# Token count in its own PSUM bank, and GpSimd work taken off the second layer's routing

## The chip, the cores and the metric

The kernel runs on one core of one Trainium2 chip. The metric is the device time of one execution in microseconds (us); before the change it was 1033.38 us, the median of three runs (1032.68 to 1035.6). In the profile, PE is the matrix engine (PEld its weight loads), DVE the vector engine, ACT the scalar engine, POOL is GpSimd, SP issues the weight loads.

## The reference, cut to what matters

512 tokens of 1024 float32 numbers pass through two layers. Each is a mixer, a layer norm, a mixture of 16 experts of which a token uses two, and another layer norm.

```python
for i in range(DEPTH):                                   # DEPTH = 2
    ...                                                  # mixer i, memory attention -> tok, xa
    o = jnp.concatenate([tok, xa], axis=-1) @ w_out[i]
    x = layer_norm(ALPHA * x + o, ln1_g[i], ln1_b[i])
    f = grouped_moe(x, router_w, router_b, w_gate[i], w_up[i], w_down[i])
    x = layer_norm(ALPHA * x + f, ln2_g[i], ln2_b[i])

# grouped_moe
scores = sigmoid(xt @ router_w); sel = scores + router_b
# the group with the largest sum of its two best sel, then its two best experts
combine = ...                                            # normalised gates, 2 per token
for e in range(N_EXPERTS):                               # 16
    h = silu(xt @ w_gate[e]) * (xt @ w_up[e])
    out = out + combine[:, e:e + 1] * (h @ w_down[e])
```

## The kernel before

**Arithmetic.** A float32 operand is used as a high part (a rounded copy, made by ACT) and a low part (value minus high part, made by DVE). Each product is three matmuls: high by high, high by low, low by high (`mm3`). Weights come in loads of 1 MB (`raw`), issued by SP in a fixed order. `Stream.split` (L155) turns one load into either two pages `split` (2 x 128x1024) or a pair `high`, `low` (128x2048). A load can start when a page is free, and the loads in flight are limited.

**Routing** (`route`, L528). After the first layer norm, the four blocks of 128 rows are written to two DRAM tensors, `x1d` (rows to gather) and `rd` (the residual to which the experts add), by DMAs on POOL's queue. PE makes the logits, and DVE ranks them in small instructions, first for blocks 0 to 2 and then for block 3. PE counts positions (`pos`). DVE compares the positions with 1 to 128 (`sel`, 128x128, by `choose`, L618), and PE multiplies `sel` by the token numbers and gates, which accumulates the table `tab`: for each of the 16 experts, up to 128 token numbers and gates. `tables` (L631) makes `idxs` and `gates` from it.

**Overflow** (`overflow`, L598). PE sums how many tokens each expert has (`cnt`), DVE compares with 128, 256 and 384 (`ovf`), sums, and writes the flags and the number `nover` of full extra blocks. All five engines read `nover` (L893) and jump over a rarely used loop (L894, `more`) if it is 0, as here. Each does so in its own order of instructions; nothing behind the jump starts before it on that engine.

**Experts** (`experts`, L651). A page `xg` of two row blocks is zeroed by POOL (L655), since a gather leaves rows without a token alone. Then POOL gathers the rows of experts 0 and 1 (L668). In layer 0, the *fillers* behind the table are the last quarter of the next layer's value projection (`va`); in layer 1 they are 8 matmuls whose results nobody uses (`warm`, L299). After the jump PE transposes `xg` (`xt`, L677), ACT and DVE make its parts `xgt`, and the expert's products follow: `ga` and `ua`, transposes `htr`, then `ya`.

**What sets the order.** Before the jump, a list scheduler places the instructions of each engine; `issue_after` forbids it to place one ahead of another. Behind the jump, `manual_schedule` keeps PE, ACT and DVE in the order of the program text. Tiles of tag "R" share one PSUM bank: `lg`, `tab` and `cnt` follow each other in it. Tag "B" has three banks.

Of the kernel before, what the change touches and what calls it, by code (L numbers as in the profile page):

```python
# [22 lines left out]
AF = mybir.ActivationFunctionType  # L23
OP = mybir.AluOpType
AX = mybir.AxisListType
ET = mybir.EngineType

P = 128
D = 1024
KB = D // P  # L30
S = 512
NC = S // P
# [3 lines left out]
E = 16  # L36
# [11 lines left out]
def trunk(ctx, tc, x, mem, w_in_a, sgu_ln_g, sgu_ln_b, sgu_w, sgu_b, w_in_b, conv_w, w_kv, w_out,  # L48
          ln1_g, ln1_b, router_w, router_b, w_gate, w_up, w_down, ln2_g, ln2_b, out):
    nc = tc.nc  # L50
    vec, act, pool_e, pe, sp = nc.vector, nc.scalar, nc.gpsimd, nc.tensor, nc.sync
# [12 lines left out]
    def page(name, shape, dtype=FT, of=None):  # L64
        of = free_pages if of is None else of
        assert of, f"no page for {name}; held: {sorted(v[1] for v in held.values())}"
        i = of.pop(0)
        uid[0] += 1
        t = pages.tile(shape, dtype, name=f"{name}_{uid[0]}", tag=f"pg{i}", bufs=1)
        held[id(t)] = (i, name, t)  # L70
        return t

    def drop(*ts):
        for t in ts:
            i, name, _ = held.pop(id(t))
            W.home(name).append(i)
# [4 lines left out]
    def bank(shape, name="bank"):  # L81
        return psum.tile(shape, FT, name=name, tag="B", bufs=3)

    def tiny(n, name):
        return psum.tile([P, n], FT, name=name, tag="R", bufs=1)


    class Half:


        def __init__(self, high, low, *pages):
            self.high, self.low, self.pages = high, low, pages
# [5 lines left out]
    class Stream:  # L98
        def __init__(self):
            self.todo, self.raw, self.ready = [], [], []  # L100
            self.keep, self.ahead, self.stop, self.sent = 0, 4, 0, 0
            self.hold, self.whole, self.count, self.on_pool = False, False, 0, lambda n: False
            self.after, self.behind, self.loads, self.flight = None, None, [], 2
            self.spare, self.parts = free_pages, 0

        def rings(self, n):
# [48 lines left out]
        def split(self):  # L155
            t, h = self.raw[0]
            if self.whole and not h:
                high, low = (page(n, [P, 4, 512], FR, self.spare) for n in ("high", "low"))
                src = t
                self.ready += [Half(high[:, 0:2], low[:, 0:2]), Half(high[:, 2:4], low[:, 2:4], high, low)]  # L160
                self.raw[0][1] = 2
            else:
                g = page("split", [P, 2, 2, 512], FR, self.spare)
                src, high, low = t[:, 2 * h:2 * h + 2], g[:, 0], g[:, 1]
                self.ready.append(Half(high, low, g))
                self.raw[0][1] += 1
            with ExitStack() if self.after is None else tc.issue_after(self.after):
                act.activation(high, src, AF.Copy)  # L168
            (pool_e if self.on_pool(self.count) else vec).tensor_tensor(low, src, high, op=OP.subtract)  # L169
            self.count += 1  # L170
            if self.raw[0][1] == 2:
                self.raw.pop(0)
                drop(t)
# [24 lines left out]
    W = Stream()  # L198

    def mm3(o, a, b, start, stop):  # L200
# [2 lines left out]
        pe.matmul(o, a[0], b[1], start=False, stop=False)  # L203
        return pe.matmul(o, a[1], b[0], start=False, stop=stop)  # L204

    def split_to(hi, lo, src):
        r = act.activation(hi, src, AF.Copy)  # L207
        vec.tensor_tensor(lo, src, hi, op=OP.subtract)  # L208
        return r


# [39 lines left out]
    ones_b = consts.tile([P, P], BF, name="ones_b")  # L251
# [16 lines left out]
    thr = consts.tile([P, 3 * E], FT, name="thr")  # L268
# [26 lines left out]
    def keep_warm(n):  # L295

        t = bank([P, 4, P], "warm")
        for _ in range(n):
            pe.matmul(t, ones_b, ones_b[:, None, :].to_broadcast([P, 4, P]), start=True, stop=True)  # L299
# [54 lines left out]
    def project_t(xh, xl):  # L354

        a = [acc("za") for _ in range(4)]
        for j in range(4):
            g = W.next()
            for kk in range(2):
                k = 2 * j + kk  # L360
                for b in range(4):
                    cs = slice(b * P, (b + 1) * P)
                    mm3(a[b], (g[:, 0, kk, cs], g[:, 1, kk, cs]), (xh[k // 4][:, k % 4, :], xl[k // 4][:, k % 4, :]),
                        k == 0, k == KB - 1)
            W.done(g)
        return a
# [141 lines left out]
    nover = consts.tile([1, 1], I32, name="nover")  # L508
# [3 lines left out]
    oh = consts.tile([P, NC, E], BF, name="oh")  # L512
# [85 lines left out]

    def overflow():

        cnt = tiny(E, "cnt")
        for c in range(NC):
            pe.matmul(cnt, ones_b, oh[:, c], start=(c == 0), stop=(c == NC - 1))
        f = small.tile([1, E, 3], FT, name="ovf", bufs=1)
        vec.tensor_tensor(f, cnt[0:1, :, None].to_broadcast([1, E, 3]),
                          thr[0:1].rearrange("p (e j) -> p e j", j=3), op=OP.is_gt)
        no = small.tile([1, 1], FT, name="ovn", bufs=1)
        vec.tensor_reduce(no, f.rearrange("p e j -> p (e j)"), axis=AX.X, op=OP.add)
        vec.tensor_copy(flags, f.rearrange("p e j -> p (e j)"))
        vec.tensor_copy(nover, no)  # L610

    tab, last_entry = [], []
    idxs = consts.tile([P, E], I32, name="idxs")
    gates = consts.tile([P, E], FT, name="gates")

# [15 lines left out]
    def tables():  # L631

        t = tab[0].rearrange("p (e t) -> p e t", t=3)
        vec.tensor_scalar(idxs, t[:, :, 0], 1.0, None, op0=OP.subtract)
        return vec.tensor_reduce(gates, t[:, :, 1:3], axis=AX.X, op=OP.add)

    def table(pp, rhs):

# [12 lines left out]
    def experts(i, lnp, fill, after, stop, fine=False):  # L651

        last = E - 1
        xg = page("xg", [P, 2, D])
        pool_e.memset(xg, 0.0)  # L655
        hy = page("h", [P, 4, FE])
        hp = hy[:, 0:2]
        xt = page("xgt", [P, 2, KB, P], FR)
# [8 lines left out]
        def gather(e):  # L667
            pool_e.indirect_dma_start(out=xg[:, e % 2], out_offset=None, in_=x1d[i],  # L668
                                      in_offset=bass.IndirectOffsetOnAxis(ap=tabs[e][0], axis=0),
                                      bounds_check=S - 1, oob_is_err=False)  # L670

        def xtrans(e):
            for q in range(2):
                t = bank([P, 4, P], "xt")
                for k in range(4):
                    k0 = 4 * P * q + 2 * P * (k // 2) + k % 2
                    pe.transpose(t[:, k, :], xg[:, e % 2, k0:k0 + 2 * P - 1:2], ident)  # L677
                split_to(xt[:, 0, 4 * q:4 * q + 4, :], xt[:, 1, 4 * q:4 * q + 4, :], t)
# [41 lines left out]
        gather(0)  # L720
        gather(1)
        if i:
            with tc.issue_after(last_entry[-1]):
                keep_warm(8)
        fill()
        more(i, hy)
# [2 lines left out]
        W.rings(8)  # L729
        xtrans(0)  # L730
        gather(2)
        W.pump()
        order = ExitStack()
        order.enter_context(tc.manual_schedule(engines={ET.PE, ET.Activation, ET.DVE}))
        for e in range(E):
# [15 lines left out]
            if e == last:  # L751
# [5 lines left out]
                t = bank([P, NC, P], "selt")  # L757
# [213 lines left out]
    stop = -len(W.todo) - W.sent  # L971
# [20 lines left out]
    t = bank([P, 12], "cwt")  # L992
    pe.transpose(t, cwr, ident[:12, :12])
    act.activation(cw.rearrange("p t b -> p (t b)"), t, AF.Copy)
    t = bank([P, H, P], "sgt")
# [7 lines left out]
    a = project_t(xh, xl)  # L1003
# [6 lines left out]
    a = project(xh, xl)  # L1010
# [5 lines left out]
    a = project_t(xh, xl)  # L1016
# [25 lines left out]
    def mixer_end(i, ch, cl, lnp):  # L1042
        lg = [tiny(3 * E, "lg"), None]

        def after(c, normed):
            if c == 0:
                W.on_pool = (lambda n: n % 2 == 1) if i == 0 else (lambda n: n % 3 != 0)
                W.keep, W.ahead = (2, 3) if i == 0 else (1, 2)
                W.pump()
            if c == NC - 1:  # L1050
                lg[1] = bank([P, E], "lg3")
                lg.append(normed)
            logits(c, i, lg[1] if c == NC - 1 else lg[0][:, c * E:(c + 1) * E])
            if c % 2:
                drop(xs[c // 2])
            if c == 1:
                W.pump()
        project_out(i, ch, cl, lnp, after)
        drop(lnp)
        rp = page("route", [P, 2048])  # L1060
        route(0, 3, lg[0].rearrange("p (n e) -> p n e", e=E), lg[2], rp)
        route(3, 1, lg[1].rearrange("p (n e) -> p n e", e=E), lg[2], rp)
        tables()
        drop(rp)
        overflow()
        W.ahead = 4

    mixer_end(0, ch, cl, lnp)
    kv1 = []
    W.keep = 6  # L1070
# [20 lines left out]
    a = project_halves(xh, xl)  # L1091
# [7 lines left out]
    a = project_t(xh, xl)  # L1099
    for h in range(H):  # L1100
        act.activation(cgp[:, h, :], a[h], AF.Copy)
    a = project_t(xh, xl)
# [7 lines left out]
    a = project_t(xh, xl)  # L1110
# [10 lines left out]
    W.keep = 3  # L1121
    mixer_end(1, ch, cl, lnp)
    W.keep = 6
    W.pump()

    def store(c):
        for n in range(2):
            ns = slice(n * 512, (n + 1) * 512)
            sp.dma_start(out[0, c * P:(c + 1) * P, ns], xrow[c][:, ns])
    experts(1, (ln2_g[1], ln2_b[1]), lambda: None, store, 0, fine=True)  # L1130


# [26 lines left out]
```

## Time and profile before

| | |
|---|---|
| median of 3 runs | 1033.38 us (1032.68 to 1035.6) |
| profiled execution, its own time | 1031.97 us |
| its span | 1030.1 us, 12721 instructions |
| PE busy | 983.7 us (95%) |
| DVE busy | 774.2 us (75%) |
| ACT busy | 627.7 us (61%) |
| POOL busy | 200.5 us (19%) |
| read from HBM | 262.22 MB |

The busy time of an engine is the sum of its instructions; matmuls are pipelined, so a busy PE can still be slow. The granted clock is a share of PE's full speed: 1.00 is 2.4 GHz, 0.50 is 1.2 GHz. The span is cut into 40 slices of 25.75 us on the page; PE is under 90% in six of them: the first, the last, one at 206 us and three from 670 to 747 us, where the experts of a layer begin.

### The profile page before, as it was taken

To read this page: it belongs to the slowest core of one execution; us is meant where nothing else is said; L and a number is where in the kernel's file an instruction comes from. 1 tells how busy PE (TensorE), PEld (TensorE's weight loads), DVE (VectorE), ACT (ScalarE), POOL (GpSimd) and SP (SyncE) were. 2 spreads that over 40 slices of the span, in tenths; PEclk is the share of its full clock that TensorE was granted. 3 is DMA by queue.
4 is the path that set the end of the run, shared out by engine and by line. 5 is a ranking of instruction groups with operands and counts; after the bars stand their busy time and mean duration, and the time that the engine had idled before them with its cause. 6 is when DMAs were issued, how large, how long until landed. Compare 5 with 4: busy or idle time off the path is not lost. (4 is left out here: it accounts for less than half of the span.)

```text
span 1030.1 us, 12721 instructions
## 1 busy us (share of the span) xinstructions
PE 983.7 (95%) x4815; PEld 810.6 (79%) x4816; DVE 774.2 (75%) x884; ACT 627.7 (61%) x684; POOL 200.5 (19%) x111
## 2 busy tenths in 40 slices
PE   8999999969999999999999999977899999999995
PEld 6788888858888888888679887865688888888873
DVE  4738567867989898898894455675689898988975
ACT  4626532556788787878643414233687887878763
POOL 0000002112332413321110000221133324233023
PEclk9999999989999999999999999987899999999998
DMA  9813266667999999999880425490799999999944
GB/s 321 294 42 123 91 237 247 244 225 265 364 367 333 366 360 360 360 357 362 282 320 1 164 82 207 131 396 25 232 330 362 372 327 383 359 362 355 357 87 160
DMA packets 102219, 273.30 MB, mean 265 GB/s; under 512 B 10442, under 2 KB 10966, under 8 KB 102152
## 3 DMA queue, kind: packets, MB, share of 16 engines
q1 hardware_dynamic: 89480, 242.84, 64.5%
q0 software_dynamic: 11808, 26.97, 9.4%
q10 hardware_dynamic: 864, 2.62, 0.7%
q8 instruction: 39, 0.64, 0.2%
q14 instruction: 28, 0.23, 0.1%
HBM read 262.22 MB, written 26.21 MB: 280 GB/s over the span
## 5 line engine op out<-in xcount | busy, mean ns | idle before, releaser
L169 DVE TENSOR_TENSOR low<-raw,high 128x2048 fp32r<-128x2048 f32 x189 | 427.9, 2288 | 80.9 <-ACT high L168 79.4
L168 ACT ACTIVATE high<-raw 128x2048 fp32r<-128x2048 f32 x189 | 355.1, 1910 | 22.7 <-PE ga L204 10.1
L668 POOL DMA_INDIRECT xg<-x1d,idxs x32 | 83.2, 2601 | 299.6 <-PE xt L677 270.5
L168 ACT ACTIVATE split<-raw 128x1024 fp32r<-128x1024 f32 x66 | 68.9, 1058 | 71.1 <-PE za L204 26.0
L202 PE MATMUL ya<-high,ht 128*128 128x512 f32 x256 | 103.8, 406 | 0.0
L169 DVE TENSOR_TENSOR split<-raw,split 128x1024 fp32r<-128x1024 f32 x61 | 73.6, 1221 | 39.6 <-ACT split L168 38.9
L204 PE MATMUL ga<-high,xgt 128*128 128x512 f32 x248 | 99.1, 399 | 2.9 <-DVE xgt L208 2.9
L204 PE MATMUL ya<-high,ht 128*128 128x512 f32 x256 | 101.3, 396 | 0.1
L203 PE MATMUL ya<-low,ht 128*128 128x512 f32 x256 | 101.1, 395 | 0.0
L202 PE MATMUL ga<-high,xgt 128*128 128x512 f32 x248 | 100.7, 406 | 0.1
L203 PE MATMUL ga<-low,xgt 128*128 128x512 f32 x248 | 98.4, 397 | 0.0
L204 PE MATMUL ua<-high,xgt 128*128 128x512 f32 x248 | 97.1, 392 | 0.0
L202 PE MATMUL ua<-high,xgt 128*128 128x512 f32 x248 | 96.9, 391 | 0.0
L203 PE MATMUL ua<-low,xgt 128*128 128x512 f32 x248 | 96.8, 390 | 0.0
L169 POOL TENSOR_TENSOR split<-raw,split 128x1024 fp32r<-128x1024 f32 x5 | 11.9, 2383 | 267.0 <-DVE sto L475 147.0
L202 PE MATMUL za<-xh,split 128*128 128x512 f32 x160 | 61.6, 391 | 2.0 <-ACT xh L207 2.0
L203 PE MATMUL za<-xl,split 128*128 128x512 f32 x160 | 62.5, 391 | 0.0
L204 PE MATMUL za<-xh,split 128*128 128x512 f32 x160 | 61.5, 389 | 0.0
L204 PEld LDWEIGHTS ga<-high,xgt 128*128 128x128 f32 x248 | 47.4, 191 | 14.1 <-DVE xgt L208 4.0
L204 PEld LDWEIGHTS ya<-high,ht 128*128 128x128 f32 x256 | 48.1, 188 | 12.8 <-DVE ht L208 1.3
L664 POOL DMA_INDIRECT rd<-h,idxs x16 | 40.4, 2523 | 89.3 <-ACT h L718 79.6
L202 PEld LDWEIGHTS ya<-high,ht 128*128 128x128 f32 x256 | 48.4, 189 | 10.5 <-ACT ht L207 0.6
(250 smaller groups left out, 1886.2 us busy)
## 6 DMA issues: line engine op xcount, KB each, us to landing
raw<-in_w_gate_dram SPq DMA_DIRECT2D x64, 1024.0 KB, 9.8
raw<-in_w_up_dram SPq DMA_DIRECT2D x64, 1024.0 KB, 9.6
raw<-in_w_down_dram SPq DMA_DIRECT2D x64, 1024.0 KB, 10.5
raw<-in_w_kv_dram SPq DMA_DIRECT2D x8, 1024.0 KB, 7.4
raw<-in_w_out_dram SPq DMA_DIRECT2D x8, 1024.0 KB, 8.0
raw<-in_w_in_b_dram SPq DMA_DIRECT2D x8, 1024.0 KB, 11.1
raw<-in_w_in_a_dram SPq DMA_DIRECT2D x6, 1024.0 KB, 5.4
x1d<-x POOLq DMA_DIRECT2D x8, 512.0 KB, 6.0
```

The costliest lines, as they stand in the source:

```text
L168: act.activation(high, src, AF.Copy)
L169: (pool_e if self.on_pool(self.count) else vec).tensor_tensor(low, src, high, op=OP.subtract)
L202: pe.matmul(o, a[0], b[0], start=start, stop=False)
L203: pe.matmul(o, a[0], b[1], start=False, stop=False)
L204: return pe.matmul(o, a[1], b[0], start=False, stop=stop)
L664: added[e] = pool_e.indirect_dma_start(out=rd[i], out_offset=bass.IndirectOffsetOnAxis(ap=tabs[e][0], axis=0), in_=ys[e % 2], in_offset=No ...
L668: pool_e.indirect_dma_start(out=xg[:, e % 2], out_offset=None, in_=x1d[i], in_offset=bass.IndirectOffsetOnAxis(ap=tabs[e][0], axis=0), bou ...
```

## The change

1. `cnt` gets a tile of tag "B" instead of sharing the bank of `tab`, so its matmuls no longer wait until `gates` has been read. In layer 1 the fillers must now come behind the last `cnt` matmul. The four DVE instructions of the count are placed behind `gates`.
2. In layer 1, ACT zeroes `xg` with a scaled copy of ones, where POOL did it.
3. In layer 1, the low parts of the splits placed around the routing are all made by DVE, behind the write of `nover`.
4. At the start of `experts`, in both layers, the low parts that `pump` makes there are placed behind the second low part of the first rows (`xgt`).

```diff
-            (pool_e if self.on_pool(self.count) else vec).tensor_tensor(low, src, high, op=OP.subtract)
+            with ExitStack() if self.low_after is None else tc.issue_after(self.low_after):
+                (pool_e if self.on_pool(self.count) else vec).tensor_tensor(low, src, high, op=OP.subtract)
...
     def split_to(hi, lo, src):
         r = act.activation(hi, src, AF.Copy)
-        vec.tensor_tensor(lo, src, hi, op=OP.subtract)
+        last_low[:] = [vec.tensor_tensor(lo, src, hi, op=OP.subtract).ins]
...
-        cnt = tiny(E, "cnt")
+        cnt = bank([P, E], "cnt")
         for c in range(NC):
-            pe.matmul(cnt, ones_b, oh[:, c], start=(c == 0), stop=(c == NC - 1))
+            m = pe.matmul(cnt, ones_b, oh[:, c], start=(c == 0), stop=(c == NC - 1))
...
+        with tc.issue_after(tabbed[0]):
+            vec.tensor_tensor(f, cnt[0:1, :, None].to_broadcast([1, E, 3]),
+                              thr[0:1].rearrange("p (e j) -> p e j", j=3), op=OP.is_gt)
...
-        vec.tensor_copy(nover, no)
+        return m.ins, vec.tensor_copy(nover, no).ins
...
-        pool_e.memset(xg, 0.0)
+        if i:
+            act.activation(xg.rearrange("p a d -> p (a d)"), ones_b[:, 0:1].to_broadcast([P, 2 * D]), AF.Copy, scale=0.0)
+        else:
+            pool_e.memset(xg, 0.0)
...
-            with tc.issue_after(last_entry[-1]):
+            with tc.issue_after(counted[0]), tc.issue_after(last_entry[-1]):
                 keep_warm(8)
...
+        W.low_after = last_low[0]
         W.pump()
+        W.low_after = None
...
     mixer_end(1, ch, cl, lnp)
     W.keep = 6
+    W.low_after, W.on_pool = counted[1], lambda n: False
     W.pump()
+    W.low_after = None
```

On DVE in layer 0, from the table to the jump, this stood before (`low` are weights of expert 0, `vt` values of the next layer's attention):

```order
L634 TENSOR_SCALAR idxs<-tab 128x16
L635 TENSOR_REDUCE gates<-tab 128x16
L169 TENSOR_TENSOR low_2081<-raw_1310,high_2080 128x2048
L169 TENSOR_TENSOR low_2057<-raw_1254,high_2056 128x2048
L208 TENSOR_TENSOR vt_1701<-va,vt_1701 128x512
L605 TENSOR_TENSOR ovf<-cnt,thr 1x48
L208 TENSOR_TENSOR vt_1701<-va,vt_1701 128x512
L608 TENSOR_REDUCE ovn<-ovf 1x1
L609 CAST flags<-ovf 1x48
L610 CAST nover<-ovn 1x1
L893 TENSOR_LOAD nover
```

In the changed kernel the same place on DVE reads:

```order
L638 TENSOR_SCALAR idxs<-tab 128x16
L639 TENSOR_REDUCE gates<-tab 128x16
L609 TENSOR_TENSOR ovf<-cnt,thr 1x48
L612 TENSOR_REDUCE ovn<-ovf 1x1
L613 CAST flags<-ovf 1x48
L614 CAST nover<-ovn 1x1
L170 TENSOR_TENSOR low_2081<-raw_1310,high_2080 128x2048
L211 TENSOR_TENSOR vt_1701<-va,vt_1701 128x512 x2
L902 TENSOR_LOAD nover
```

The count moved ahead of one `low` and both `vt`; the other `low` went behind the jump and behind both `xgt` low parts. With it one load of SP, which reuses that page, went behind the jump.

On POOL in layer 1, from the last rows to the jump, this stood before:

```order
L516 DMA x1d_114<-x_4275 128x1024
L517 DMA rd_116<-x_4275 128x1024
L169 TENSOR_TENSOR split_5889<-raw_5061,split_5889 128x1024
L655 MEMSET xg_5892 128x2048
L668 DMA xg_5892<-x1d_114,idxs 128x1024 x2
L893 TENSOR_LOAD nover
```

In the changed kernel it is this:

```order
L519 DMA x1d_114<-x_4275 128x1024
L520 DMA rd_116<-x_4275 128x1024
L675 DMA xg_5892<-x1d_114,idxs 128x1024 x2
L902 TENSOR_LOAD nover
L903 COMPARE_AND_BRANCH
```

The split and the memset left POOL; the memset stands on ACT between `split_5889` and a `high`, and the gathers now wait for ACT.

On DVE in layer 1, the end of the routing in the changed kernel:

```order
L622 TENSOR_SCALAR sel<-slot_91,pos_99 128x128 x2
L597 TENSOR_TENSOR route_5781<-route_5781 128x32
L598 CAST tok<-route_5781 128x32
L599 TENSOR_TENSOR tok<-route_5781,tok 128x32
L638 TENSOR_SCALAR idxs<-tab 128x16
L639 TENSOR_REDUCE gates<-tab 128x16
L609 TENSOR_TENSOR ovf<-cnt,thr 1x48
L612 TENSOR_REDUCE ovn<-ovf 1x1
L613 CAST flags<-ovf 1x48
L614 CAST nover<-ovn 1x1
L170 TENSOR_TENSOR split_5886<-raw_5061,split_5886 128x1024
L170 TENSOR_TENSOR split_5889<-raw_5061,split_5889 128x1024
```

Both splits are new here. `split_5886` stood ahead of the last layer norm's mean before:

```order
L474 SCALAR_TENSOR_TENSOR x_4275<-x_4275,oa 128x512
L475 BN_STATS sto_5387<-x_4275 128x6
L169 TENSOR_TENSOR split_5886<-raw_5061,split_5886 128x1024
L458 BN_AGGR mv<-sto_5387 128x2
L460 TENSOR_SCALAR ve<-mv 128x1
L463 SCALAR_TENSOR_TENSOR x_4275<-x_4275,mv,ln_5380 128x1024
```

It left this place; `split_5889` came from POOL.

## Rows read from the trace of the kernel before

**Rows 1.** Windows of stretches: us, PE, PEld, DVE, ACT, POOL busy; granted clock; DMA share; GB/s.

```profile
205.90:213.40 7.50, 0.13 (x5) 0.03 (x2) 5.97 (x8) 1.06 (x2) 0.68 (x1) 0.83 0.86 261
213.40:217.60 4.20, 4.17 (x14) 3.44 (x15) 1.38 (x2) 2.02 (x3) 0.99 (x1) 0.50 0.91 338
...
231.60:235.00 3.40, 3.40 (x8) 2.69 (x9) 3.33 (x3) 0.27 (x1) 0.19 (x1) 0.53 0.90 289
...
724.20:733.10 8.90, 7.73 (x20) 5.76 (x21) 6.29 (x5) 4.62 (x6) 0.00 (x0) 0.50 0.81 266
```

**Rows 2.** Timeline, layer 0: start, us, engine, line, out<-in, count, [idle before <-releaser].

```profile
203.24 0.18 DVE L635 TENSOR_REDUCE gates<-tab 128x16 f32<-128x32 f32 x1
204.17 1.08 POOL L668 DMA_INDIRECT xg<-x1d,idxs  x1 [22.48 <-DVE gates L635]
...
205.56 1.02 POOL L668 DMA_INDIRECT xg<-x1d,idxs  x1 [0.30 <-issue]
...
205.80 4.50 DVE L169 TENSOR_TENSOR low<-raw,high 128x2048 fp32r<-128x2048 f32 x2 [2.38 <-ACT high L168]
...
211.73 0.14 DVE L610 CAST nover<-ovn 1x1 int32<-1x1 f32 x1
...
213.43 1.95 PE L677 MATMUL xt<-ident,xg 128*128 128x128 f32 x8 [7.40 <-DVEq L894]
```

**Rows 3.** DMA issues, us to landing: the gathers of 204.17, 205.56 and 701.36.

```profile
xg<-x1d,idxs POOLq DMA_INDIRECT x1, 4.2
...
xg<-x1d,idxs POOLq DMA_INDIRECT x1, 6.2
...
xg<-x1d,idxs POOLq DMA_INDIRECT x1, 4.3
```

**Rows 4.** Timeline of layer 1's routing, all engines.

```profile
680.50 1.21 DVE L169 TENSOR_TENSOR split<-raw,split 128x1024 fp32r<-128x1024 f32 x1
...
690.90 2.34 POOL L169 TENSOR_TENSOR split<-raw,split 128x1024 fp32r<-128x1024 f32 x1 [4.96 <-ACT split L168]
690.96 4.39 DVE L618 TENSOR_SCALAR sel<-slot,pos 128x128 fp32r<-128x128 f32 x3
...
693.47 1.80 POOL L655 MEMSET xg<- 128x2048 f32 x1 [0.23 <-DMA rd<-x]
...
696.06 0.17 DVE L564 SCALAR_TENSOR_TENSOR route<-route 128x16 f32<-128x16 f32 x1
...
700.50 0.18 DVE L635 TENSOR_REDUCE gates<-tab 128x16 f32<-128x32 f32 x1
...
701.36 1.08 POOL L668 DMA_INDIRECT xg<-x1d,idxs  x1 [6.09 <-DVE gates L635]
...
704.48 0.13 DVE L610 CAST nover<-ovn 1x1 int32<-1x1 f32 x1
...
706.02 1.95 PE L677 MATMUL xt<-ident,xg 128*128 128x128 f32 x8 [2.12 <-PEq L894]
```

**Rows 5.** Timeline: three comparisons in layer 0, and layer 1's fillers.

```profile
195.21 0.67 DVE L618 TENSOR_SCALAR sel<-slot,pos 128x128 fp32r<-128x128 f32 x3
...
700.20 3.61 PE L299 MATMUL warm<-ones_b 128*128 128x512 bf16 x8
```

**Rows 6.** Timeline: two gathers of layer 0's experts, and a low part beside one.

```profile
334.59 2.29 DVE L169 TENSOR_TENSOR low<-raw,high 128x2048 fp32r<-128x2048 f32 x1
334.61 3.18 POOL L668 DMA_INDIRECT xg<-x1d,idxs  x1 [9.07 <-PE xt L677]
...
370.43 1.03 POOL L668 DMA_INDIRECT xg<-x1d,idxs  x1 [9.07 <-PE xt L677]
```

**Rows 7.** A load late in layer 0's experts, the copies that read it, loads' time to landing.

```profile
459.78 0.37 SPq L147 DMA_DIRECT2D raw<-in_w_down_dram  x1
...
470.01 3.71 ACT L168 ACTIVATE high<-raw 128x2048 fp32r<-128x2048 f32 x2
...
raw<-in_w_down_dram SPq DMA_DIRECT2D x1, 1024.0 KB, 10.4
```

More of the change, by code (lines that the diff above doesn't have):

```diff
@@ L102, in __init__ @@
             self.hold, self.whole, self.count, self.on_pool = False, False, 0, lambda n: False
-            self.after, self.behind, self.loads, self.flight = None, None, [], 2
+            self.after, self.low_after, self.behind, self.loads, self.flight = None, None, None, [], 2
             self.spare, self.parts = free_pages, 0
@@ L204, in mm3 @@
         return pe.matmul(o, a[1], b[0], start=False, stop=stop)
+    last_low = []
     def split_to(hi, lo, src):
         r = act.activation(hi, src, AF.Copy)
-        vec.tensor_tensor(lo, src, hi, op=OP.subtract)
+        last_low[:] = [vec.tensor_tensor(lo, src, hi, op=OP.subtract).ins]
         return r
@@ L599, in overflow @@
     def overflow():
-        cnt = tiny(E, "cnt")
+        cnt = bank([P, E], "cnt")
         for c in range(NC):
-            pe.matmul(cnt, ones_b, oh[:, c], start=(c == 0), stop=(c == NC - 1))
+            m = pe.matmul(cnt, ones_b, oh[:, c], start=(c == 0), stop=(c == NC - 1))
         f = small.tile([1, E, 3], FT, name="ovf", bufs=1)
-        vec.tensor_tensor(f, cnt[0:1, :, None].to_broadcast([1, E, 3]),
-                          thr[0:1].rearrange("p (e j) -> p e j", j=3), op=OP.is_gt)
+        with tc.issue_after(tabbed[0]):
+            vec.tensor_tensor(f, cnt[0:1, :, None].to_broadcast([1, E, 3]),
+                              thr[0:1].rearrange("p (e j) -> p e j", j=3), op=OP.is_gt)
         no = small.tile([1, 1], FT, name="ovn", bufs=1)
@@ L609, in overflow @@
         vec.tensor_copy(flags, f.rearrange("p e j -> p (e j)"))
-        vec.tensor_copy(nover, no)
-    tab, last_entry = [], []
+        return m.ins, vec.tensor_copy(nover, no).ins
+    tab, last_entry, counted, tabbed = [], [], [], []
     idxs = consts.tile([P, E], I32, name="idxs")
@@ L634, in tables @@
         vec.tensor_scalar(idxs, t[:, :, 0], 1.0, None, op0=OP.subtract)
-        return vec.tensor_reduce(gates, t[:, :, 1:3], axis=AX.X, op=OP.add)
+        tabbed[:] = [vec.tensor_reduce(gates, t[:, :, 1:3], axis=AX.X, op=OP.add).ins]
     def table(pp, rhs):
@@ L1064, in mixer_end @@
         drop(rp)
-        overflow()
+        counted[:] = overflow()
         W.ahead = 4
```

## Prediction

> **What bounds the kernel now.** I read the busy shares first: PE works 95% of the span, so time can only be won where it waits. The windows over the whole span show three such places: the start, the end, and the first 40 us of each layer's experts. The change touches the last. There I read the timeline of all engines, and from it who ended each wait.
>
> Layer 0: PE finishes its fillers at about 206.0 and starts the transposes of expert 0's rows at 213.43; in the 7.5 us between it is busy 0.13 us [rows 1, 2]. What it waits for is `nover`, written at 211.73 + 0.14 = 211.87; reading it and jumping takes 213.43 − 211.87 = 1.56 us. The reader is to see that `nover` depends on nothing heavy: `gates` is there at 203.42, but the DVE queue has two low parts (4.50 us, themselves waiting until 205.80) and two `vt` ahead of the end of the count [rows 2]. The gathered rows of expert 0 landed long before: issued at 204.17, 4.2 us to landing, so 208.37 [rows 2, 3].
>
> Layer 1: `gates` ends at 700.68, the gather is issued at 701.36 and lands 4.3 us later at 705.66, and PE starts at 706.02, 0.36 us behind it [rows 3, 4]. `nover`, written at 704.48 + 0.13 = 704.61, would by the 1.56 us above allow 706.17, by what was seen at most 706.02: both arrive together, and both must come earlier for a gain. What makes `gates` late is seen in the same rows: three comparisons `sel` take 4.39 us of elapsed time, while the same three take 0.67 in layer 0 [rows 4, 5]. They start at 690.96, 0.06 us after POOL's split, and end only after POOL's memset has ended at 695.27. DVE was held by POOL; without POOL's work there is nothing to hold it.
>
> This contention is what the Trainium skill describes in "SBUF — State Buffer", section "Who interferes with whom": VectorE and GpSimd share one pair of ports, a lock that the first takes for a whole instruction. The trace agrees: 4.39 against 0.67 us.
>
> **Layer 0, step by step.** In the new order the four count instructions follow `gates` directly. They are as small as `gates` and `nover` themselves, 0.14 to 0.18 us each, 0.7 in a row [rows 2], so `nover` is ready at about 204.1, while PE is still in its fillers. PE can then be through the jump at 206.0 + 1.56 = 207.6 at the latest. Now the gather is late next: 208.37 + 0.36 = 208.7. PE's restart moves from 213.43 to 208.7: **4.7 us**. DVE must be through its own jump when the low part of the rows is wanted. It still does one low part from 205.80 to 208.05 and two `vt` (1.35 us) to 209.4; with 1.0 to 1.56 us for the jump it is free at 210.4 to 211.0, and by the distances of before it is wanted 1.8 us after the restart, at 210.5. So this costs 0 to 0.5 us. Bounds: 4.2 (that 0.5 counts in full) to 5.8 (the landing does not hold PE, 207.6). I take 4.7, because the landing has a row of its own.
>
> The low part moved behind the jump (2.29 us) now runs beside expert 0's first products. Twenty-four matmuls stand ahead of its first reader, and the first 4.2 us after the restart hold only 14 instructions including the transposes [rows 1], so it is hidden; without that cover it would cost up to 2.3 us. The weight load that reuses its page goes out some 4 us later, at about 214.3 instead of 210.3; it is one of the loads that wait tens of us before use, so nothing.
>
> **Layer 1, step by step.** (a) Without `split_5886` ahead of the last norm's mean, the norm of block 3 comes 1.1 us earlier (1.21 us less the overlap) [rows 4]. The routing of blocks 0 to 2 gains less, since ACT's table load and sigmoid are then late next, but the positions wait for block 3's logits on PE, which follow the norm. I take 1.0; one more small DVE instruction now stands between positions and `sel`, −0.15. Bounds 0.3 to 1.1. (b) From the first `sel` at 690.96 to the instruction behind the sixth, 696.06, pass 5.1 us. Undisturbed it is two batches of 0.67 and two small instructions, 1.5 to 1.7 us: gain 3.5. Bounds 2.7, if the table matmuls, at half clock here, feed the buffers of `sel` slowly, to 3.6. (c) The three early `cnt` matmuls stand in PE's queue ahead of the table, about 0.1 us while `sel` is still being made: nothing. (d) Zeroing by ACT, put at the 1.86 us that ACT takes for a 128x2048 copy (half of 3.71, [rows 7]): it waits, like the memset before, for the last rows' store to `rd`, which ended at 693.47 and goes out 1.0 earlier. So it runs from 692.5 to 694.4; the gather comes at about 697.0. A `high` part behind it is not wanted for ten more us. Hidden, with 2.6 us to spare; beyond that it costs one for one. So `gates` comes 1.0 − 0.15 + 3.5 = 4.35 us earlier.
>
> (e) What the change puts in the way: the splits (1.21 us each) now stand on DVE right behind `nover`, that is 0.7 to 0.8 us after the start of `gates`, and the gather is issued 0.86 us after it [rows 4]. In the experts a gather issued 0.02 us after the start of a 2.29 us low part took 3.18 us, that is until its end plus 0.9; another in nearly the same position took 1.03 [rows 6]. So a gather that comes just behind is held until the first split ends: 1.21 − 0.15 + 0.9 instead of 1.08, or **0.9 us** late. Bounds: 0 if it comes first, 2.1 if the second split holds it too. I take 0.9, the common case of the experts' gathers.
>
> Here the same page and section of the Trainium skill speaks the other way: a `tensor_tensor` should only hinder GpSimd's reads, and generating DMA descriptors is inferred to need the write side alone. By it (e) costs nothing; 3.18 against 1.03 us speaks against it.
>
> Then PE restarts at 706.02 − 4.35 + 0.9 = 702.6. The jump does not hold it: the fillers end at 703.81 − 4.35 = 699.5, plus 1.56 gives 701.0. **3.45 us**, bounds 0.9 to 4.7.
>
> **Sum.** 4.7 + 3.45 = 8.15 us. Everything behind a restart follows PE at the same distances (the order on DVE, ACT and SP is unchanged there), so both gains reach the end. Against the profiled execution: 1031.97 − 8.15 = 1023.8. That execution was 1.4 us under the median of the timed runs; for the median I take 1033.38 − 8.15 = **1025.2 us**. Its own range is 1023.5 to 1027.
>
> **Rivals.**
> *More.* In the 7.5 us wait the granted clock averages 0.83 and it is 0.50 for the 4.2 us after it [rows 1]; in the changed kernel the wait is 2.7 us. If PE keeps 2.4 GHz over it, the transposes and six matmuls are some 1.6 us shorter. Against it: the stretch at 0.53 from 231.6 follows a wait too, of under 2 us [rows 1]. With it, or with the gather not held (0.9), the time is 1022.7 to 1024.3, for both 1022.7.
>
> *Weights late.* A load issued at 459.78 is read by the copies from 470.01 on, the second of which starts at 471.9: 12.1 us, of which 10.4 to land [rows 7]. If PE comes 4.7 us earlier and the loads do not, layer 0's gain is gone before its end: 1025.2 + 4.7 = 1029.9. Against it: early in the experts loads are released by DVE's low parts, which move with PE.
>
> *The change does not reach layer 0.* If the first transposes wait for both gathers, the second lands at 205.56 + 6.2 = 211.76 and PE starts at 212.1: a gain of 1.3 there, 1028.6 in all. Against it: in layer 1 PE started at 706.02, only 4.66 us after the first issue and 3.3 after the second's (one gather and 0.3 us later).
>
> *Slower.* PE's clock. After a restart it works at half clock for 4.2 us in layer 0, and after the wait at 720 us in layer 1 for 8.9 us [rows 1]. A matmul then takes 0.43 instead of 0.23 us. The fillers of layer 1 run at half clock too (3.61 us for 8, [rows 5]), so they do not raise it. If in the new rhythm the splits keep interrupting PE, half clock can persist over the first experts; from 56 matmuls more at that rate (24 us) on, 11.2 us are lost and the kernel is 3.1 us slower, 1036.5. For it: the stretch of 8.9 us exists. Against it: it ends by itself, and the order that makes it is the same.
>
> **How the numbers follow.** Forecast 0.56; more 0.20; weights late 0.08; layer 0 not reached 0.11; slower 0.05. The range that holds 8 in 10 is 1021.5 to 1029.5: it takes in the forecast's bounds, "more" with 1 us of scatter between runs, and the unreached layer 0. A measurement here tells no more than 0.3%, 3.1 us, from no change. Weights late (3.5 us of gain) lies on that line, so half of its 0.08 is counted as the same, with 0.03 of the unreached layer 0: faster 0.88, same 0.07, slower 0.05.
>
> **What would show it.** Layer 0: `nover` within 1 us of `gates`, PE's first `xt` about 5.5 us after `gates` starts, not 10.2. Layer 1: three `sel` in under 0.8 us, no POOL work between the rows' stores and the gather; the gather over 1.5 us long if (e) is right; PE's first `xt` 6.4 us after `gates` starts (5.5 if not held). Wrong: an `xt` that starts 1.4 to 1.6 us after `nover` again, a PE wait on a low part or a load in the experts that before has none, or half-clock stretches that grow by more than 10 us in sum.

## The result and the profile after

The changed kernel takes 1024.85 us (median of 6 runs, 1023.47 to 1026.41); the kernel before took 1031.85 us beside it (6 runs, the three shown ahead among them). The ratio is 0.9933, with a 95% interval of 0.9917 to 0.9949: 5.3 to 8.6 us faster. The profiled execution took 1024.8 us, with a span of 1023.1 us against 1030.1.

The same stretches of the windows as in [rows 1], moved with the work: the wait in layer 0, the transposes and the products behind them, the stretch a little later, and the one in layer 1. The clock is the third number from the end.

```profile
205.90:209.40 3.50, 0.04 (x1) 0.00 (x0) 3.40 (x3) 1.88 (x2) 0.65 (x1) 1.00 0.74 214
209.40:210.80 1.40, 1.19 (x8) 1.03 (x8) 0.00 (x0) 0.59 (x2) 0.00 (x0) 0.92 0.93 328
210.80:214.00 3.20, 3.14 (x7) 2.44 (x8) 3.16 (x3) 0.67 (x3) 0.99 (x1) 0.50 0.98 336
...
227.60:231.00 3.40, 3.40 (x9) 2.62 (x10) 3.22 (x3) 0.16 (x1) 0.09 (x1) 0.51 0.91 301
...
716.50:725.50 9.00, 7.15 (x18) 5.37 (x19) 6.92 (x7) 4.72 (x6) 0.00 (x0) 0.50 0.74 252
```

The wait of 7.5 us has become one of 3.5, at full clock throughout, and the stretches at half clock are all still there. In the 3.5 us it is VectorE that works: 3.40 us busy. The timeline of layer 0 says with what [rows 2].

```profile
203.21 0.18 DVE L639 TENSOR_REDUCE gates<-tab 128x16 f32<-128x32 f32 x1
...
203.75 0.14 DVE L614 CAST nover<-ovn 1x1 int32<-1x1 f32 x1
...
204.14 1.08 POOL L675 DMA_INDIRECT xg<-x1d,idxs  x1 [22.45 <-DVE nover L614]
...
205.81 2.29 DVE L170 TENSOR_TENSOR low<-raw,high 128x2048 fp32r<-128x2048 f32 x1 [1.91 <-PE va L204]
...
208.02 1.28 DVE L211 TENSOR_TENSOR vt<-va,vt 128x512 fp32r<-128x512 f32 x2
...
209.46 1.19 PE L684 MATMUL xt<-ident,xg 128*128 128x128 f32 x8 [3.52 <-DVEq L903]
...
212.04 2.28 DVE L170 TENSOR_TENSOR low<-raw,high 128x2048 fp32r<-128x2048 f32 x1
...
217.86 0.39 PE L203 MATMUL ga<-high,xgt 128*128 128x512 f32 x1
```

`nover` is ready 0.7 us behind the start of `gates`, in place of 8.6. The transposes start at 209.46, 3.97 us earlier than before, and 0.16 us after the second `vt` has ended (208.02 + 1.28 = 209.30). What they waited for stands in the brackets: `DVEq L903`, VectorE's queue at the jump. The moved low part runs from 212.04 to 214.32, and the earliest products that can need it start 3.5 us behind that.

Layer 1's routing on all engines answers to [rows 4] and, with `sel`, to [rows 5]; the zeroing is ScalarE's.

```profile
685.80 0.67 DVE L622 TENSOR_SCALAR sel<-slot,pos 128x128 fp32r<-128x128 f32 x3
...
687.30 0.17 DVE L567 SCALAR_TENSOR_TENSOR route<-route 128x16 f32<-128x16 f32 x1
688.38 1.91 ACT L660 ACTIVATE xg<-ones_b 128x2048 f32<-128x2048 bf16 x1 [3.21 <-DVE route L554]
...
691.73 0.18 DVE L639 TENSOR_REDUCE gates<-tab 128x16 f32<-128x32 f32 x1
692.35 0.14 DVE L614 CAST nover<-ovn 1x1 int32<-1x1 f32 x1
692.41 2.34 DVE L170 TENSOR_TENSOR split<-raw,split 128x1024 fp32r<-128x1024 f32 x2
692.59 3.11 POOL L675 DMA_INDIRECT xg<-x1d,idxs  x1 [11.73 <-DVE nover L614]
...
699.13 1.95 PE L684 MATMUL xt<-ident,xg 128*128 128x128 f32 x8 [4.09 <-DMA xg<-x1d,idxs]
```

Three `sel` take 0.67 us in place of 4.39. But the first gather takes 3.11 us in place of 1.08: it starts 0.18 us behind the two splits and ends 0.95 us after both (692.41 + 2.34 = 694.75). PE restarts 6.89 us earlier than before.

The profiled executions differ by up to 3.9 us in when they reach layer 0's routing at all (`gates` at 203.08 to 206.93), so distances between marks are compared below. That scatter goes with PE's clock, ahead of everything that the edits touch: before, changed, e1 and e4 keep 1.00 up to there, e5, e6 and e7 fall to half clock once (0.66 from 40 to 45 us in e6), e2 and e3 also from 26 to 30 (0.57), and each fall goes with an arrival some 1.8 us later. Each distance is worked out from starts in the timelines, in us; "end" is the span's. The column from `sel` is a part of the one before it.

| kernel | median | ratio, interval | `gates` 0 to `xt` 0 | `xt` 0 to `gates` 1 | of it, `sel` to `gates` | `gates` 1 to `xt` 1 | `xt` 1 to end |
|---|---|---|---|---|---|---|---|
| before | 1031.85 | 1 | 10.19 | 487.07 | 9.54 | 5.52 | 324.08 |
| changed | 1024.85 | 0.9933 [0.9917, 0.9949] | 6.25 | 482.27 | 5.93 | 7.40 | 323.97 |
| e1 | 1028.42 | 0.9970 [0.9956, 0.9984] | 6.22 | 486.99 | 9.61 | 5.38 | 324.17 |
| e2 | 1028.88 | 0.9973 [0.9956, 0.9990] | 8.41 | 483.95 | 5.94 | 7.46 | 323.92 |
| e3 | 1023.49 | 0.9921 [0.9899, 0.9942] | 6.23 | 482.32 | 5.94 | 5.48 | 323.14 |
| e4 | 1024.39 | 0.9934 [0.9913, 0.9954] | 4.97 | 483.50 | 5.92 | 7.64 | 323.71 |
| e5 | 1020.88 | 0.9898 [0.9874, 0.9922] | 5.02 | 480.50 | 5.93 | 5.43 | 323.16 |
| e6 | 1026.41 | 0.9949 [0.9935, 0.9964] | 6.25 | 482.18 | 6.87 | 7.57 | 323.77 |
| e7 | 1026.53 | 0.9949 [0.9933, 0.9965] | 6.21 | 484.47 | 5.93 | 6.44 | 323.69 |

### The profile page after: what moved, and what is told of

Its sections match the earlier page's. It is cut to its first block, busy times and chain, and to the rows that moved or that the text cites. A ratio compares the mean times of both kernels' runs of the same rounds, so it can differ in the third digit from the quotient of the medians.

```text
span 1023.1 us, 12720 instructions
## 1 busy us (share of the span) xinstructions
PE 982.4 (96%) x4815; PEld 809.3 (79%) x4816; DVE 771.3 (75%) x885; ACT 629.8 (62%) x685; POOL 200.6 (20%) x109
## 5 line engine op out<-in xcount | busy, mean ns | idle before, releaser
L675 POOL DMA_INDIRECT xg<-x1d,idxs x32 | 87.4, 2731 | 300.8 <-PE xt L684 261.7
L170 POOL TENSOR_TENSOR split<-raw,split 128x1024 fp32r<-128x1024 f32 x4 | 9.6, 2390 | 262.1 <-DVE sto L478 147.0
```

## The experiments

All start from the changed kernel; e1 takes layer 1's part of the change out of it, e5 joins e3 and e4, the others turn one thing. The kernel before ran beside each: 1031.85 us with the changed kernel, 1031.19 with e1 to e4, 1032.05 with e5 to e7.

**e1, the count and the moved low part alone.**

```
-        if i:
-            act.activation(xg..., ones_b..., AF.Copy, scale=0.0)
-        else:
-            pool_e.memset(xg, 0.0)
+        pool_e.memset(xg, 0.0)
...
-    W.low_after, W.on_pool = counted[1], lambda n: False
     W.pump()
-    W.low_after = None
```

> The changed kernel with layer 1's GpSimd work put back: the split on GpSimd, the memset on GpSimd, and the other split ahead of the last norm, as before. What is left of the change is the count in its own bank ahead of the fillers, and the low part behind the first rows. Theory (layer 0's gain is the early count, layer 1's is GpSimd taken off the selectors): layer 0 restarts at 209.5 as in the changed kernel, 4.0 us earlier than before; in layer 1 three sel take about 4.4 us again and PE restarts some 4.0 us earlier than 706.02, at 702.0; 4.0 us below the kernel before in all, 1027.9. Rival (layer 1 gained from its early count, and GpSimd does not hold VectorE): sel takes 0.7, or PE restarts near 699.1 in spite of it; 7 us below, 1024.9.

Measured: the theory. Layer 0 keeps its 3.97 us (10.19 to 6.22), layer 1 has none. From layer 0's `gates` to the end the profiles differ by 4.1 us; the medians differ by 2.8, with an interval of 1.6 to 4.5. The timeline of VectorE and GpSimd shows `sel` held again:

```profile
687.09 2.34 POOL L170 TENSOR_TENSOR split<-raw,split 128x1024 fp32r<-128x1024 f32 x1 [4.96 <-ACT split L168]
689.52 1.81 POOL L659 MEMSET xg<- 128x2048 f32 x1
...
687.14 4.33 DVE L622 TENSOR_SCALAR sel<-slot,pos 128x128 fp32r<-128x128 f32 x3
```

It also divides layer 1's gain. `sel` starts 477.38 us behind the restart of layer 0 here (687.14 − 209.76) and 476.34 in the changed kernel (685.80 − 209.46): 1.04 us is the split taken from ahead of the norm. The norm shows it directly: from the start of its sum (`x<-x,oa`) to the start of its mean (`mv`) pass 2.46 us here, 2.45 before, and 1.45 in the changed kernel and all others. Whether it reaches `sel` hangs on the clock over the logits in between (see e4). From `sel` to `gates` pass 9.61 and 5.93: 3.68 us is GpSimd, split and memset together.

**e2, the low part back ahead of the jump.**

```
-        W.low_after = last_low[0]
         W.pump()
-        W.low_after = None
```

> The changed kernel with layer 0's low part back ahead of the jump (two low parts and two vt behind nover on VectorE; one weight load goes out ahead of the jump too). Theory (PE's first transposes wait until VectorE has done all that stands ahead of its own jump): 2.29 us more of VectorE work, so PE's first xt in layer 0 at 211.7 instead of 209.46, and 2.2 us above the changed kernel, 1027.1. Rival (PE waits for the gathered rows to land): xt stays at 209.5 and the time at 1024.9.

Measured: `xt` 2.16 us later, so VectorE's queue is what PE waits for, not the rows. Timeline of layer 0:

```profile
209.32 4.49 DVE L170 TENSOR_TENSOR low<-raw,high 128x2048 fp32r<-128x2048 f32 x2 [1.88 <-PE va L204]
213.73 1.28 DVE L211 TENSOR_TENSOR vt<-va,vt 128x512 fp32r<-128x512 f32 x2
...
215.17 1.95 PE L684 MATMUL xt<-ident,xg 128*128 128x128 f32 x8 [5.72 <-DVEq L901]
```

Again PE starts 0.16 us after `vt` has ended (215.01). The total is 4.0 us over the changed kernel, not 2.2. The rest, 1.68 us up to layer 1's `gates`, goes with the clock: 0.94 of it up to the transposes of layer 1's tokens for the logits (`rt`, the last but eight), 0.73 from those to `sel`, where the clock falls early as in e4. The windows behind the restart:

```profile
215.10:217.00 1.90, 1.83 (x9) 1.63 (x9) 0.07 (x1) 0.60 (x1) 0.00 (x0) 0.50 0.95 321
217.00:222.00 5.00, 5.00 (x15) 3.91 (x15) 1.35 (x3) 2.51 (x2) 0.99 (x1) 0.60 0.84 329
```

The clock fell within the longer wait, so the transposes take 1.95 us again and not 1.19, and it is still low 5 us later.

**e3, the gather ahead of the splits.**

```
-    def overflow():
+    def overflow(pads):
...
-        return m.ins, vec.tensor_copy(nover, no).ins
+        r = vec.tensor_copy(nover, no)
+        for _ in range(pads):
+            with tc.issue_after(r.ins):
+                r = vec.tensor_copy(flags, f.rearrange("p e j -> p (e j)"))
+        return m.ins, r.ins
...
-        counted[:] = overflow()
+        counted[:] = overflow(4 * i)
```

`i` is the layer, 0 or 1: layer 0 gets no copies.

> The changed kernel with four more copies of the flags (about 0.12 us each) on VectorE behind layer 1's nover, so that the two splits start 0.4 to 0.5 us later, after the first gather has started. Theory (the splits hold the gather's descriptor writing until both have ended): the first gather takes about 1.05 us instead of 3.11, PE's first xt in layer 1 comes 2.0 us earlier against gates, 6.4 to 5.4 us behind it, and the kernel is 2.0 us below the changed one, 1022.8. Rival (the gather is slow for another reason, the DMA queue or the store of the rows): it takes 3.1 us again, the time is 1024.9 or up to 0.5 more.

Measured: the theory. Timeline of layer 1 behind `nover`:

```profile
696.10 0.13 DVE L614 CAST nover<-ovn 1x1 int32<-1x1 f32 x1
696.21 0.81 DVE L617 CAST flags<-ovf 1x48 int32<-1x48 f32 x4
696.35 1.07 POOL L679 DMA_INDIRECT xg<-x1d,idxs  x1 [11.74 <-DVE nover L614]
696.94 2.34 DVE L170 TENSOR_TENSOR split<-raw,split 128x1024 fp32r<-128x1024 f32 x2
...
697.72 2.47 POOL L679 DMA_INDIRECT xg<-x1d,idxs  x1 [0.30 <-issue]
```

The splits start 0.84 us behind the start of `nover`, in place of 0.06. The gather that now comes first takes 1.07 us, though the splits start before its end; now the second gather stands behind them and takes 2.47, but nothing waits for it. `gates` to `xt` falls from 7.40 to 5.48. Behind the shorter wait the transposes run at full clock (1.00 from 700.9 to 702.2, 1.20 us in place of 1.95 at 0.50), which is most of the 0.83 us by which `xt` to the end is shorter. Four small copies that compute nothing new make the kernel 1.4 us faster by the medians, 1.2 by the ratios; the two intervals overlap, so what tells is the 1.92 us of the distance.

**e4, both low parts behind the first rows.**

```
         W.low_after = last_low[0]
         W.pump()
-        W.low_after = None
...
+            if e == 1:
+                W.low_after = None
             up = gate_up(e, ...)
```

> The changed kernel with layer 0's other low part behind the first rows too, so that only two vt stand on VectorE between nover and its jump (one weight load moves behind the jump with it). Theory (PE waits for VectorE's jump): vt end at about 207.4, then the gathered rows are late next, landing at 208.24; PE's first xt at 208.6 instead of 209.46, 0.8 us below the changed kernel, 1024.0. Rival (the rows' landing holds PE already): xt stays at 209.5, 1024.9. A loss, if the up products wait for the low part that now comes last: up to 2.3 us, 1027.2.

Measured: `xt` 1.28 us earlier against `gates`, more than the 0.8 expected, and now it is the rows it waits for (the gather of 204.01 took 3.9 us to landing, to 207.91):

```profile
205.80 1.37 DVE L211 TENSOR_TENSOR vt<-va,vt 128x512 fp32r<-128x512 f32 x2 [2.03 <-ACT vt L210]
...
208.05 1.20 PE L684 MATMUL xt<-ident,xg 128*128 128x128 f32 x8 [2.24 <-DMA xg<-x1d,idxs]
```

Yet the time is the changed kernel's: 0.9934 against 0.9933. No wait took the gain: in the two profiles PE restarts layer 0 1.41 us earlier (208.05 and 209.46) and keeps 1.30 of it through all experts, to the transposes of layer 1's tokens (`rt`, the last but eight, 675.72 and 677.02), but layer 1's `gates` comes only 0.18 us earlier. In between, the logits ran slower. Windows of the changed kernel over them:

```profile
676.00:678.00 2.00, 2.00 (x21) 2.00 (x20) 1.93 (x4) 1.13 (x4) 0.00 (x0) 1.00 1.02 419
678.00:680.00 2.00, 1.75 (x16) 1.68 (x16) 1.63 (x4) 1.78 (x3) 0.20 (x1) 1.00 1.03 420
680.00:682.00 2.00, 1.75 (x15) 1.51 (x13) 1.79 (x7) 1.08 (x2) 0.86 (x2) 0.90 1.02 412
```

And of e4:

```profile
676.00:678.00 2.00, 2.00 (x17) 2.00 (x15) 1.96 (x3) 1.59 (x2) 0.00 (x0) 0.75 1.03 418
678.00:680.00 2.00, 2.00 (x11) 2.00 (x11) 0.93 (x4) 0.60 (x3) 1.05 (x2) 0.50 1.03 420
680.00:682.00 2.00, 2.00 (x11) 1.76 (x9) 1.76 (x8) 1.10 (x2) 0.00 (x0) 0.50 1.01 410
```

The clock falls 4 to 5 us earlier, although the same work comes only 1.3 us earlier. It is not e4's edit alone: from `rt` to `sel` pass 9.91 us here, 9.75 in e5, 9.51 in e2 and 9.48 in e6, but 8.78 in the changed kernel and 8.77 in e3, with the same work in between. Why the clock falls earlier in some of them is open.

**e5, e3 and e4 together.**

> The two edits of e3 (four copies between nover and the splits) and e4 (both low parts behind the first rows) together. In e4 PE restarted layer 0 1.28 us earlier against gates and kept it to the last norm of layer 1 (1.30 us at its last transposes but eight), and lost 1.1 of it in layer 1's logits, where its matmuls went at half clock earlier than in the changed kernel. Theory (the two gains are independent, and where the clock falls is e4's only loss): PE's first xt 5.0 us behind gates in layer 0 and 5.5 in layer 1; 1022.2 if the clock falls where it fell in the changed kernel, 1023.3 if it falls early again. Rival (e4's edit gains nothing at all): 1023.5 with the clock falling as late as in the changed kernel.

Measured: both gains, in every distance (5.02 and 5.43), and the best time of the study, 1020.88 us. It lies under all figures expected. In its profile the clock did not fall at all behind the restart of layer 0: from there to `rt` pass 464.82 us, in place of 467.56. Windows from the wait on:

```profile
207.80:210.10 2.30, 0.02 (x1) 0.02 (x1) 1.37 (x2) 1.80 (x2) 0.63 (x1) 1.00 0.60 123
210.10:211.50 1.40, 1.20 (x8) 1.01 (x8) 0.01 (x1) 0.72 (x3) 0.00 (x0) 1.00 1.01 401
211.50:217.00 5.50, 5.49 (x23) 4.27 (x24) 5.50 (x4) 3.18 (x3) 0.99 (x1) 1.00 0.56 149
```

In layer 1 it fell early, as in e4 (0.61 from 676 to 678), and took 1.0 of it back. e4, whose layer 0 is the same program with the same wait, fell to half clock behind the restart and e5 did not: as far as two profiles tell, that is a matter of the run and not of the edit.

**e6, the zeroing back on GpSimd.** The edit is e1's upper half.

> The changed kernel with layer 1's zeroing back on GpSimd, the splits as changed. The memset takes 1.80 us and starts when the rows' store to rd has landed, about 688.4, so it lies beside the routing of block 3. Theory (it holds VectorE's sel alone): sel of block 3 ends at 690.4 instead of 690.3, gates 0.3 us later at most, 1025.1. Rival one (it holds any VectorE instruction): all of the small routing instructions from 688.5 on wait until 690.2, gates 1.6 us later, 1026.5. Rival two (it holds none, and sel was slow for another reason): 1024.9 with sel at 0.28 us each.

Measured: neither theory nor rivals. The time is close to rival one's 1026.5, but not for its reason: `sel` to `gates` grew by 0.94 us, not 1.6, and one instruction explains it:

```profile
688.70 1.80 POOL L659 MEMSET xg<- 128x2048 f32 x1 [7.66 <-PE tab L631]
688.81 0.18 DVE L552 SCALAR_TENSOR_TENSOR route<-route,before 128x16 f32<-128x16 f32 x1
689.02 0.17 DVE L554 SCALAR_TENSOR_TENSOR route<-route 128x16 f32<-128x16 f32 x1
689.23 0.17 DVE L556 TENSOR_REDUCE route<-route 128x4 f32<-128x16 f32 x1
689.43 1.10 DVE L572 TENSOR_SCALAR route<-route 128x4 f32<-128x4 f32 x1
```

The memset lets two kinds of instruction pass and holds the first `TENSOR_SCALAR`, of four columns, until its own end (690.50). `sel` is a `TENSOR_SCALAR` too; here six of them came before the memset and two after it. The distance from layer 0's restart to `gates` did not grow in this profile, because the clock stayed at 1.00 from 226 to 234, where the changed kernel had 0.71 and 0.87. The timed runs are 1.6 us above the changed kernel's, with overlapping intervals; what tells is the instruction.

**e7, one split back on GpSimd.**

```
-    W.low_after, W.on_pool = counted[1], lambda n: False
+    W.low_after = counted[1]
```

> The changed kernel with one of layer 1's two splits back on GpSimd; the zeroing stays on ScalarE, the other split behind nover. Theory: GpSimd's split runs from 685.2 for 2.34 us, the first sel at 685.80 is held until 687.5, gates 1.7 us later; one split only stands beside the first gather, which takes about 2.0 us instead of 3.11; PE's first xt 6.3 us behind gates instead of 7.4; in sum 0.6 us later than the changed kernel, 1025.5. Rival one (only the memset held sel): sel at 0.28 us each and 1.1 us below the changed kernel, 1023.8. Rival two (the gather's length is not the splits'): it takes 3.1 us again, 1026.6.

Measured: both halves of the theory, but the instruction held is another. Timeline of layer 1:

```profile
687.10 2.33 POOL L170 TENSOR_TENSOR split<-raw,split 128x1024 fp32r<-128x1024 f32 x1 [4.51 <-ACT split L168]
687.21 2.31 DVE L552 SCALAR_TENSOR_TENSOR route<-route,before 128x64 f32<-128x64 f32 x1
...
689.64 0.67 DVE L622 TENSOR_SCALAR sel<-slot,pos 128x128 fp32r<-128x128 f32 x3
...
696.25 1.20 DVE L170 TENSOR_TENSOR split<-raw,split 128x1024 fp32r<-128x1024 f32 x1
696.43 1.98 POOL L675 DMA_INDIRECT xg<-x1d,idxs  x1 [7.00 <-DVE nover L614]
```

GpSimd's split held not `sel` but an instruction with two inputs ahead of it, for 2.31 us; `sel` starts 2.2 us later against the restart (478.54 in place of 476.34). With one split ahead of it the gather takes 1.98 us, the 1.2 us of the split less 0.15, and 0.9: the prediction's own sum for that case. Up to PE's restart in layer 1 the two come to 1.2 us of loss, where 0.6 was expected; the medians show 1.7, with overlapping intervals.

## Why the prediction was right, and where it was not

The time was right (1025.2 forecast, 1024.85 measured), and in the main so was the mechanism; one step in layer 0 was not, and one term in layer 1 had half its size. The terms came to 8.15 us, the traces show 6.89 at the restart of layer 1 and 7.0 at the end. That the number still fits to 0.4 us is luck: the forecast was reckoned from a median of before over three runs, which came down by 1.5 us with three more.

- **Layer 0, 4.7 forecast, 3.94 to 3.97 measured, just under its bounds.** The count behind `gates`, the fillers' end and the end of `vt` (209.4 forecast, 209.30 measured) came as worked out. The step that failed is "now the gather is late next". VectorE's own jump was, and it holds PE's first transpose, not only the low part of the rows; so it is counted from the transposes and not from 1.8 us later. In return it costs 0.16 us behind `vt`, not 1.0 to 1.56, since VectorE's sequencer reads `nover` while the engine is still at work. What read `nover`, and when, in the changed kernel's layer 0 (the last two times are the first and the last start):

```profile
L902 PEldq TENSOR_LOAD <-nover x1: 488/488/488, 203.9 to 203.9; - x1
...
L902 DVEq TENSOR_LOAD <-nover x1: 541/541/541, 206.6 to 206.6; - x1
```

  VectorE's reading at 206.6 lies inside its low part. Who then advanced a semaphore (a counter on which others wait) at the jump, line 903, and when:

```profile
L903 DVEq EVENT_SEMAPHORE  x2: 21/21/21, 209.3 to 209.4; - x2
...
L903 SPq COMPARE_BRANCH x1: 45/45/45, 209.1 to 209.1; - x1
```

  VectorE advances its own behind its last `vt`, right ahead of PE's start. SyncE is late at its jump too (209.1), but advances none there before PE starts, so it is not what PE waits for. Nor is it a PSUM bank that `vt` frees: in the kernel's text `xt` has tag B and `va` tag A. e2 (one low part more, 2.16 us later) and e4 (one fewer, 1.28 earlier, then the rows) show it by experiment. The row of before names VectorE's queue as well (`<-DVEq L894`, [rows 2]), but could not tell the two apart: there `nover` came last of all.
- **The moved low part: nothing, as forecast.** It ended 3.5 us ahead of its earliest reader. The load that reuses its page went out at 217.75, not at 214.3, and PE waited for no load.
- **Layer 1, (a) and (b): 4.35 forecast, 4.8 measured.** (a) 1.04 in place of 0.85 net, by e1, with the clock over the logits alike; (b) 3.6 to 3.7 in place of 3.5: from the first `sel` to the instruction behind the sixth pass 1.50 us (685.80 to 687.30), as forecast. e6 and e7 show that each of GpSimd's two instructions costs VectorE time here by itself: 0.94 and 2.1 to 2.2 us where they then fall.
- **(d): nothing, as forecast.** Zeroing ended at 690.29, 2.3 us ahead of the gather; its 1.91 us match the 1.86 taken from the copies [rows 7].
- **(e): 0.9 forecast, 1.9 to 2.0 measured, within its bounds of 0 to 2.1.** This is the mis-sized term, and the bound that the prediction gave for it (the second split holds it too) is what happened. The gather waits not for the first split but for both, as they follow without a gap: 3.11 us with two splits, 1.98 with one (e7), 1.07 with none (e3). Between the 8.15 and the 6.89, this takes 1.0 and layer 0 0.7, and (a) with (b) gave 0.45 back.
- **The rule that spoke against (e).** The trace says that a `tensor_tensor` of VectorE holds the gather, e3 and e7 for one and two splits. The Trainium skill, "SBUF — State Buffer", section "Who interferes with whom", infers that descriptor generation needs the write side alone; the measurement decides, and here it is wrong for a gather that takes its rows from a list in SBUF. Its rule on what two-input instructions contend with fits e6 and e7: a memset reads nothing and let two-input instructions pass, a split reads and held one, and a `TENSOR_SCALAR` was held by the memset.
- **The rivals.** "More" half came: PE kept 2.4 GHz over the wait and the transposes (1.19 us in place of 1.95), then fell for the 3.2 us after them, so of 4.36 us at the first product 4.03 were left at the transposes of expert 2 (239.65 and 243.68). Weights late: no wait for a load appears, and from `xt` 0 to `gates` 1 e1 keeps the distance of before (486.99 and 487.07). Layer 0 not reached: PE waits for one gather only (e4: 208.05, long before the second, issued at 205.40, which took 6.5 us to landing in the changed kernel). Slower: the stretches at half clock are about as long as before (3.2, 3.4 and 9.0 us, in place of 4.2, 3.4 and 8.9).

## What to carry to other kernels

When the last of several waits is taken away, work out for every engine at the jump when it is through. Here the next to end was VectorE's jump, 0.8 us behind the rows that had been reckoned with, and the row of before had named its queue. Where VectorE works beside an indirect gather of GpSimd, their order counts: 0.8 us of small copies put ahead of two splits brought 1.9 us, because the gather then came first and was not held. And a gain of a microsecond or two at a restart is only certain after the next stretch at half clock, which can give as much again (e5) or take it (e4, e2).

## What the runs showed of the hardware that was not expected

Beside a memset on GpSimd a `TENSOR_SCALAR` of VectorE with four columns took 1.10 us in place of 0.17, until the memset's end, while two-input instructions and a reduction of 16 columns passed at their usual 0.17 to 0.18 us (e6). Beside GpSimd's split a two-input instruction of VectorE took 2.31 us in place of 0.21 (e7). Two splits of VectorE in a row held a gather until the second had ended (3.11 us).

PE's clock differed between kernels whose work around it is the same: after a wait of 2.2 to 2.3 us it fell behind the transposes in e4 and stayed at 2.4 GHz in e5, 1.3 us of difference by the transposes of expert 1 (13.97 us after the restart in e4, 12.69 in e5) and 2.9 by those of expert 2 (30.31 and 27.42). Executions of one kernel differ in it too: the kernel before took 1028.90 us at a mean granted clock of 0.978, and 1035.15 at 0.969. What decides it was not tried.
